# Retention over running streams: state blocks of two sequences, grouped query-state products and stores from GpSimd's queue

## The chip, the core and the metric

The kernel runs on one core of one Trainium2 chip. The metric is the device time of one execution in microseconds (us), the median of several runs. The core has a matrix engine (TensorE, PE in the profile, with its weight loads as PEld), VectorE (DVE), ScalarE (ACT), GpSimd (POOL) and SyncE (SP, which here only issues DMAs), and 16 DMA engines that all queues share.

## What is computed

The reference is one inference step of a two-layer streaming trunk. Layer 0 is multi-scale retention, layer 1 a gated spatial unit, and each is followed by a gated ConvFFN. There are 512 prompt rows of one new stream and 16 rows each of 8 running streams (the samples), 640 rows in all, with 1024 features. The change lies in the retention alone, 4 heads with keys of 256 and values of 512. Every sample has a running state S of 256 x 512 for each head; its part of one head is

```
scores = einsum('blhd,bshd->bhls', q, k) * intra
o = einsum('bhls,bshe->blhe', scores, v)
o = o + einsum('blhd,bhde->blhe', q * q_dec, S)
S = S * exp(L * log_gamma) + einsum('blhd,blhe->bhde', k * k_dec, v)
```

The third line is the query-state product, the fourth makes the new state, which is an output (ret_sample), as is the new state of the prompt (ret_prompt).

## The kernel before

Activations are held transposed (features on partitions), the rows split into a half of 384 and one of 256. Every weight block is loaded, cut into two exact parts (wh by ScalarE, wl by VectorE, `split_w`, line 63) and multiplied in three passes. `retention` (line 507) goes through four heads. For each head it makes queries and keys (`ret_qk`), values (`ret_v`), the inner part (`ret_inner`, line 642), the gate (`ret_gate`, line 738, whose products carry the name prow, as those of `ret_v` do), turns the result (`ret_turn`, pyT) and multiplies it by the output weights (`ret_out`, pxA and pxB). Blocks of the conditioning vectors (`ada`, tile pada, line 297) are put in between, one or two with each weight block.

`ret_inner` first makes the samples' scores times values (into the PSUM bank pos) and the prompt's new state in two halves (pS, copied to so at line 665, stored at 666). Then come four rounds, one for each pair of `par` (odd or even sequences) and `dt` (half of the keys). A round handles four sequences:

- it loads four state blocks of 128 x 512 (256 KB each, line 675) into tiles s0 (s in the profile);
- it adds four query-state products to pos (line 678), each with 32 columns of stationary queries, to partitions 0, 32, 64 or 96 of the same bank; the matrix engine is used in four column tiles of 128 x 32 there;
- for each pair of sequences it multiplies 48 rows of keys by values (psn, line 695; the operands st were stored to DRAM as sk and sv and loaded again in another layout, lines 689 and 690), and VectorE updates the state in place (line 696);
- each new state is stored (line 697), from SP's queue;
- one block of the prompt's attention follows (psc, then pr, ph and pl, then po).

The tiles s0 and so share one group of five buffers, so a load waits until the store of the state that used its buffer has landed. An update in place also waits until the query-state product has read the tile.

Nothing in the source fixes the order of instructions on an engine. The framework orders every engine's instructions when the program is built, by the dependences and its own estimates, and the engine then executes them in that order; so the products of a round stand between products of the gate. In this order PE stands at a wait, with all that is behind it. SP issues all loads and, before the change, all of these stores, in one order too.

Of the kernel before, what the change touches and what calls it, by code (L numbers as in the profile page):

```python
# [23 lines left out]
T = 16  # L24
# [12 lines left out]
class Trunk:  # L37
# [25 lines left out]
    def split_w(self, src, kt, cols, eng=None):  # L63
        """Load a weight block and cut it into two exact f32r parts."""
        n = kt * cols
        self.trickle(self.rates.pop(0) if self.rates else self.rate)
        raw = self.ahead.pop(0) if self.ahead else self.load_w(src, kt, cols)
        hi = self.wp.tile([128, 1024], F32R, tag="wh", name="wh")
        lo = self.wp.tile([128, 1024], F32R, tag="wl", name="wl")
        self.nc.scalar.copy(hi[:, :n], raw[:, :n])  # L70
        (eng or self.nc.vector).tensor_tensor(lo[:, :n], raw[:, :n], hi[:, :n].bitcast(F32), op=ALU.subtract)  # L71
        v = lambda t: t[:, :n].rearrange("p (k c) -> p k c", k=kt)
        return v(hi), v(lo)
# [12 lines left out]
    def w8(self, w, c0, cols=256):  # L86
        """A [1024, cols] column block of w as 8 K-tiles of (hi, lo)."""
        out = []
        for kh in range(2):
            hi, lo = self.split_w(w[kh * 512:(kh + 1) * 512, c0:c0 + cols], 4, cols)  # L90
            out += [(hi[:, k], lo[:, k]) for k in range(4)]
        return out
# [17 lines left out]
    def mm3(self, out, w, h, start, stop):  # L110
        """One K-tile of a product with stationary w, in three exact-part passes."""
        self.mm(out, w[0], h[0], start, False)
        self.mm(out, w[0], h[1], False, False)
        self.mm(out, w[1], h[0], False, stop)

    def mm3_ws(self, pA, pB, w, h, start, stop):
        """The same for both row halves."""
        whi, wlo = w
        hAh, hAl, hBh, hBl = h
        self.mm(pA, whi, hAh, start, False)  # L120
        self.mm(pB, whi, hBh, start, False)
        self.mm(pA, whi, hAl, False, False)
        self.mm(pB, whi, hBl, False, False)
        self.mm(pA, wlo, hAh, False, stop)
        self.mm(pB, wlo, hBh, False, stop)

# [1 line left out]
    def setup(self):  # L128
# [10 lines left out]
        # per-feature vectors as per-partition columns  # L139
# [14 lines left out]
        with self.tc.tile_pool(name="setup", bufs=1, reuse_waits="tile") as sp:  # L154
# [71 lines left out]
            def after(h, d0):  # L226
                """K-tiles d0 and d0 + 1 of the first queries and keys, first row half."""
# [22 lines left out]
    def ada_pair(self, dp, pool):  # L250
        """Shift and scale of the first sub-layer for two column tiles."""
# [26 lines left out]
    def ada(self, l, m):  # L278
        """Conditioning vectors of 2048 features, as steps of one weight block each."""
# [40 lines left out]
    def square(self, half, d, quick=False):  # L320
        """Adds the squares of column tile d of x to the running sum of a half."""
# [12 lines left out]
    def norm_rstd(self, half):  # L334
        """rstd of each row of a half, rows on partitions: [128, blocks]."""
# [14 lines left out]
    def norm(self, l, which, lazy=None, after=None):  # L350
        """h = rmsnorm(x) * A + B per feature and sequence, as exact f32r parts.

        Returns the result lists and a function that emits one row half."""
# [92 lines left out]
    def residual_b(self, l, gbase, d, pB, final=True):  # L446
# [5 lines left out]
        t = self.tp.tile([128, 128], F32, tag="rest", name="rest")  # L452
# [10 lines left out]
    # row block rb of h, K-tile k: (hi, lo) stationary operands  # L463
# [5 lines left out]
    def proj_rows(self, h, w, rb):  # L469
        """Row-layout product of row block rb with a [1024, 256] weight block."""  # L470
        pb = self.bank("prow")
        for k in range(KD):
            hh, hl = self.hrow(h, k, rb)
            whi, wlo = w[k]
            self.mm(pb[:, :256], hh, whi, k == 0, False)
            self.mm(pb[:, :256], hh, wlo, False, False)
            self.mm(pb[:, :256], hl, whi, False, k == KD - 1)
        return pb

    def proj_cols(self, h, w, i):  # L480
        """Transposed product with column tile i of a [1024, 256] weight block."""
# [7 lines left out]
    def proj_half(self, h, w, i, half):  # L489
        """The same for one row half."""  # L490
# [8 lines left out]
    def proj_set(self, h, ws, split):  # L499
        """Column tiles of several blocks; with split, all first halves come first."""  # L500
# [38 lines left out]
    def ret_first(self, h):  # L539
        """Rotated queries and keys of the first head, from products begun before."""  # L540
# [10 lines left out]
    def ret_qk(self, h, base, hd):  # L551
        """Rotated queries or keys of a head, transposed."""
# [20 lines left out]
    def ret_v(self, h, hd, between):  # L573
        """Values of a head in row layout, as exact f32r parts."""
# [15 lines left out]
    def ret_probs(self, hd, dtab, pb, n, c0):  # L590
        """Decayed scores in exact f32r parts."""
# [9 lines left out]
    def ret_keys(self, hd, k, dt, sk):  # L601
        """Decayed k rows, for one half of d, in exact f32r parts."""
# [20 lines left out]
    def ret_prep(self, hd, qk):  # L623
        """What the samples and the states need of queries and keys alone."""
# [4 lines left out]
        # samples: scores, and the decayed queries for the running states  # L629
# [12 lines left out]
    def ret_inner(self, hd, qk, v, prep):  # L642
# [12 lines left out]
        # the prompt state, one half of d at a time  # L655
        for dt in range(2):
# [7 lines left out]
            so = rp.tile([128, DV], F32, tag="s0", name="so", bufs=5)  # L664
# [5 lines left out]
        for rnd in range(4):  # L670
            par, dt = divmod(rnd, 2)
            s0 = []
            for i in range(4):
                t = rp.tile([128, DV], F32, tag="s0", name="s0", bufs=5)
                nc.sync.dma_start(t, io["state_ret"][0, 2 * i + par, hd, dt * 128:(dt + 1) * 128, :])
                s0.append(t)
            for i in range(4):
                nc.tensor.matmul(
                    pos[32 * i:32 * i + 32, :], self.qd[:, dt, 2 * i + par, :], s0[i], start=False, stop=True,
                    skip_group_check=True,  # L680
                )
            for pair in range(2):
# [8 lines left out]
                for i in range(2):  # L691
                    b = 2 * (2 * pair + i) + par
                    t = s0[2 * pair + i]
# [3 lines left out]
                    nc.sync.dma_start(io["ret_sample"][0, b, hd, dt * 128:(dt + 1) * 128, :], t)  # L697
            # prompt: block i of queries against key blocks i, i - 1, ..., 0
# [39 lines left out]
    def ret_gate(self, h, hd, o, last):  # L738
# [6 lines left out]
        for n, (e, rb) in enumerate(order):  # L745
# [9 lines left out]
            else:  # L755
                sg = rp.tile([128, 256], F32, tag="sg", name="sg", bufs=5)
# [5 lines left out]
    def ret_turn(self, hd, o):  # L762
        """Gated output of a head, transposed, in exact f32r parts; one row half a call."""
# [22 lines left out]
    def ret_out(self, l, hd, yT, turn, mid):  # L786
        """Adds the head's share of the output product."""
# [27 lines left out]
    def down(self, l, gbase, w, tiles, mid):  # L815
        """x += gate * (tiles^T w): tiles are [128, 640] f32, split just before use."""
# [14 lines left out]
        for d0, nd in ((0, 2), (2, 3), (5, 3)):  # L831
# [21 lines left out]
            # the last K-tiles: all of the first row half, then the second  # L853
# [104 lines left out]
    def conv_out(self, l):  # L958
        """The last raw rows of each sequence, transposed back."""
# [14 lines left out]
    def sgu(self, l, h, emit, mid):  # L974
# [16 lines left out]
        with self.tc.tile_pool(name="gp", bufs=1, reuse_waits="tile") as gp:  # L991
            # masked mixing matrices, transposed; block-diagonal ones for the samples
# [15 lines left out]
            # v in row layout  # L1008
# [137 lines left out]
def _tables():  # L1146
    """Constants that depend on the shapes alone."""
# [50 lines left out]
```

## Time and profile before

| | |
|---|---|
| median of 3 runs | 2327.37 us (2323.67 to 2332.08) |
| span of the profiled execution, first to last instruction | 2326.8 us |
| mean granted clock of TensorE | 0.988 |
| PE busy | 2239.1 us (96%) |
| PEld, DVE, ACT, POOL busy | 2086.2, 1227.8, 861.7, 432.9 us |
| DMA | 252.86 MB, mean 109 GB/s |

Of the profiled execution only the span is given, not a time of its own; the median of the runs is 0.6 us above the span. In the rows, x64 is a count of instructions, the number after "|" is the time in which at least one of them was running, then the mean of one in ns, then the idle time of the engine just before them with what ended it. A 32-bit float product, as those into pos, psc and pada are, shows as two records each; one on exact parts (prow, psn, po) shows as one. Starts and durations of a matmul are in us; the end is modelled, so the start of the next instruction says more than the duration.

### The profile page before, as it was taken

To read this page: it belongs to the slowest core of one execution; us is meant where nothing else is said; L and a number is where in the kernel's file an instruction comes from. 1 tells how busy PE (TensorE), PEld (TensorE's weight loads), DVE (VectorE), ACT (ScalarE), POOL (GpSimd) and SP (SyncE) were. 2 spreads that over 40 slices of the span, in tenths; PEclk is the share of its full clock that TensorE was granted. 3 is DMA by queue.
4 is the path that set the end of the run, shared out by engine and by line. 5 is a ranking of instruction groups with operands and counts; after the bars stand their busy time and mean duration, and the time that the engine had idled before them with its cause. 6 is when DMAs were issued, how large, how long until landed. Compare 5 with 4: busy or idle time off the path is not lost. (4 is left out here: it accounts for less than half of the span.)

```text
span 2326.8 us, 39734 instructions
## 1 busy us (share of the span) xinstructions
PE 2239.1 (96%) x15832; PEld 2086.2 (90%) x15832; DVE 1227.8 (53%) x2458; ACT 861.7 (37%) x1783; POOL 432.9 (19%) x695
## 2 busy tenths in 40 slices
PE   6999999999999999999999999699999999999998
PEld 5868968969968999999999999699999899999998
DVE  5425426326338544446656336953655664445753
ACT  4312212212214544445544222122544454445544
POOL 3201001001004322212012002770001232222010
PEclk9999999999999999999999999899999999999999
DMA  8465454262352343444322222342122122222221
GB/s 277 133 204 173 151 190 132 73 197 87 98 178 89 118 145 129 136 145 130 89 75 65 92 73 71 71 98 75 55 73 74 61 92 73 73 80 73 73 70 59
DMA packets 193009, 252.86 MB, mean 109 GB/s; under 512 B 11648, under 2 KB 158064, under 8 KB 192824
## 3 DMA queue, kind: packets, MB, share of 16 engines
q1 hardware_dynamic: 190616, 245.35, 33.1%
q0 software_dynamic: 2208, 4.98, 1.4%
q8 instruction: 124, 2.03, 0.4%
q14 instruction: 61, 0.50, 0.1%
HBM read 221.65 MB, written 28.60 MB: 108 GB/s over the span
## 5 line engine op out<-in xcount | busy, mean ns | idle before, releaser
L71 DVE TENSOR_TENSOR wl<-wr,wh 128x1024 fp32r<-128x1024 f32 (+1 forms) x284 | 351.5, 1238 | 217.1 <-ACT wh L70 214.4
L70 ACT CAST wh<-wr 128x1024 fp32r<-128x1024 f32 (+1 forms) x286 | 284.7, 995 | 434.3 <-PE pB L61 175.2
L61 PE MATMUL pA<-hi,wh 128*128 128x384 f32 x1024 | 353.5, 345 | 0.3 <-ACT hi L425 0.3
L61 PE MATMUL pA<-lo,wh 128*128 128x384 f32 x1024 | 349.0, 341 | 1.5 <-POOL lo L427 1.5
L61 PE MATMUL pA<-hi,wl 128*128 128x384 f32 x1024 | 348.2, 341 | 0.0
L61 PE MATMUL prow<-wh,hi 128*128 128x256 f32 x1072 | 306.4, 287 | 1.0 <-ACT wh L70 0.8
L61 PE MATMUL prow<-wh,lo 128*128 128x256 f32 x1072 | 305.9, 286 | 0.1
L61 PE MATMUL prow<-wl,hi 128*128 128x256 f32 x1072 | 305.8, 286 | 0.0
L61 PE MATMUL pB<-lo,wh 128*128 128x256 f32 x1024 | 287.7, 281 | 1.3 <-DVE lo L427 1.2
L61 PE MATMUL pB<-hi,wh 128*128 128x256 f32 x1024 | 287.0, 281 | 0.4 <-DVE rt L569 0.2
L61 PE MATMUL pB<-hi,wl 128*128 128x256 f32 x1024 | 286.6, 280 | 0.0
L61 PEld LDWEIGHTS prow<-wh,hi 128*128 128x128 f32 x1072 | 204.6, 191 | 19.4 <-issue 16.4
L61 PEld LDWEIGHTS prow<-wl,hi 128*128 128x128 f32 x1072 | 205.1, 191 | 16.6 <-issue 16.0
L61 PEld LDWEIGHTS prow<-wh,lo 128*128 128x128 f32 x1072 | 205.2, 191 | 16.1 <-issue 15.5
L61 PEld LDWEIGHTS pA<-hi,wh 128*128 128x128 f32 x1024 | 194.1, 190 | 10.5 <-issue 5.8
L61 PEld LDWEIGHTS pA<-lo,wh 128*128 128x128 f32 x1024 | 194.0, 189 | 3.1 <-POOL lo L427 2.5
L61 PEld LDWEIGHTS pB<-lo,wh 128*128 128x128 f32 x1024 | 193.6, 189 | 2.8 <-DVE lo L427 2.1
L61 PEld LDWEIGHTS pA<-hi,wl 128*128 128x128 f32 x1024 | 193.4, 189 | 1.4 <-issue 0.5
L61 PEld LDWEIGHTS pB<-hi,wh 128*128 128x128 f32 x1024 | 193.4, 189 | 1.0 <-DVE rt L569 0.4
L61 PEld LDWEIGHTS pB<-hi,wl 128*128 128x128 f32 x1024 | 193.3, 189 | 0.0
L61 PE MATMUL dA<-ghi,wh 128*128 128x384 f32 x544 | 185.3, 341 | 0.0
L61 PE MATMUL dA<-ghi,wl 128*128 128x384 f32 x544 | 184.6, 339 | 0.0
(227 smaller groups left out, 4293.2 us busy)
## 6 DMA issues: line engine op xcount, KB each, us to landing
wr<-in_ffn_w_up SPq DMA_DIRECT2D x88, 512.0 KB
wa<-in_w_ada SPq DMA_DIRECT2D x80, 512.0 KB
wr<-in_ret_w_in SPq DMA_DIRECT2D x48, 512.0 KB
wr<-in_sgu_w_in SPq DMA_DIRECT2D x48, 512.0 KB
wr<-in_ffn_w_down SPq DMA_DIRECT2D x44, 384.0 KB
s<-in_state_ret SPq DMA_DIRECT2D x64, 256.0 KB
out_ret_sample<-s SPq DMA_DIRECT2D x64, 256.0 KB
wr<-in_sgu_w_out SPq DMA_DIRECT2D x24, 384.0 KB
```

Source lines behind the costliest of these rows:

```text
L61: self.last_mm = self.nc.tensor.matmul(out, l, r, start=start, stop=stop).ins
L70: self.nc.scalar.copy(hi[:, :n], raw[:, :n])
L71: (eng or self.nc.vector).tensor_tensor(lo[:, :n], raw[:, :n], hi[:, :n].bitcast(F32), op=ALU.subtract)
```

## The change

- The four state blocks of a round become two tiles of 128 x 2 x 512 (512 KB each), one load for two sequences. Their group has three buffers; so moves to the shared group t2.
- The four query-state products are written with sequence 2 first, then 3, and 0 and 1 are held behind 3 on PE by an added dependence (`issue_after`).
- The new states of a pair are stored by one DMA, from GpSimd's queue.
- Two buffers are taken away elsewhere (rest 2 to 1, sg 5 to 4). All else in the diff is comments, left out here.

```diff
@@ residual_b
-        t = self.tp.tile([128, 128], F32, tag="rest", name="rest")
+        t = self.tp.tile([128, 128], F32, tag="rest", name="rest", bufs=1)
@@ ret_inner
-            so = rp.tile([128, DV], F32, tag="s0", name="so", bufs=5)
+            so = self.tp.tile([128, DV], F32, tag="t2", name="so", bufs=3)
...
             s0 = []
-            for i in range(4):
-                t = rp.tile([128, DV], F32, tag="s0", name="s0", bufs=5)
-                nc.sync.dma_start(t, io["state_ret"][0, 2 * i + par, hd, dt * 128:(dt + 1) * 128, :])
+            part = lambda a, pair: a[0].rearrange("(p i two) h d e -> p two h d i e", two=2, i=2)[
+                pair, par, hd, dt * 128:(dt + 1) * 128
+            ]
+            for pair in range(2):
+                t = rp.tile([128, 2, DV], F32, tag="s0", name="s0", bufs=3)
+                nc.sync.dma_start(t, part(io["state_ret"], pair))
                 s0.append(t)
-            for i in range(4):
-                nc.tensor.matmul(
-                    pos[32 * i:32 * i + 32, :], self.qd[:, dt, 2 * i + par, :], s0[i], start=False, stop=True,
-                    skip_group_check=True,
-                )
+
+            def read_state(i):
+                return nc.tensor.matmul(
+                    pos[32 * i:32 * i + 32, :], self.qd[:, dt, 2 * i + par, :], s0[i // 2][:, i % 2], start=False,
+                    stop=True, skip_group_check=True,
+                ).ins
+
+            read_state(2)
+            with self.tc.issue_after(read_state(3)):
+                read_state(0)
+                read_state(1)
...
                 for i in range(2):
-                    b = 2 * (2 * pair + i) + par
-                    t = s0[2 * pair + i]
+                    t = s0[pair][:, i]
                     pb = self.sbank("psn")
                     self.mm(pb, st[pair][:, i, dt * 128:(dt + 1) * 128], st[pair][:, i, DK:], True, True)
                     nc.vector.scalar_tensor_tensor(t, t, g16, pb, op0=ALU.mult, op1=ALU.add)
-                    nc.sync.dma_start(io["ret_sample"][0, b, hd, dt * 128:(dt + 1) * 128, :], t)
+                nc.gpsimd.dma_start(part(io["ret_sample"], pair), s0[pair])
@@ ret_gate
-                sg = rp.tile([128, 256], F32, tag="sg", name="sg", bufs=5)
+                sg = rp.tile([128, 256], F32, tag="sg", name="sg", bufs=4)
```

The built programs show how the order moves. On PE, second head, first round, before: the third and the fourth product of the round (pos from an s0 tile and the queries qd), with products of the gate (prow, from parts wh, wl of the weights and hi, lo of the activations) between them.

```order
L678 MATMUL pos_3155<-s0_3217,qd_922 32x512
L61 MATMUL prow_3536<-wh_3504,lo_793 128x256
L61 MATMUL prow_3536<-wh_3504,hi_800 128x256
L61 MATMUL prow_3536<-wl_3505,hi_800 128x256
L61 MATMUL prow_3536<-wh_3504,lo_801 128x256
L61 MATMUL prow_3563<-wh_3498,hi_321 128x256
L61 MATMUL prow_3563<-wl_3499,hi_321 128x256
L678 MATMUL pos_3155<-s0_3219,qd_922 32x512
L61 MATMUL prow_3563<-wh_3498,lo_322 128x256
```

After the change, on PE in the second head, its first round and then its second:

```order
L609 MATMUL pk_3153<-ident_75,qk_2744 128x128
L683 MATMUL pos_3131<-s0_3191,qd_922 32x512 x2
L683 MATMUL pos_3131<-s0_3189,qd_922 32x512
L609 MATMUL pk_3157<-ident_75,qk_2744 128x128 x4
L683 MATMUL pos_3131<-s0_3189,qd_922 32x512
L61 MATMUL prow_3460<-wh_3450,hi_321 128x256
```

```order
L61 MATMUL prow_3515<-wh_3456,lo_801 128x256
L683 MATMUL pos_3131<-s0_3234,qd_922 32x512 x2
L683 MATMUL pos_3131<-s0_3232,qd_922 32x512 x2
L61 MATMUL prow_3542<-wh_3450,hi_836 128x256
```

In the first round of a head three products now stand together and the fourth behind four transposes (pk), ahead of the prompt's second state half; in the other three rounds all four stand together. Over the four heads the order before has 56 products alone and 4 pairs; now it has 12 groups of four, 4 of three and 4 alone. Of the 64 psn products, 28 stood alone and 18 in pairs; now 40 stand alone and 12 in pairs.

On SP, second head, before, from the end of the first round to the third (s0 loads, ret_sample stores, st operands):

```order
L697 DMA out_ret_sample<-s0_3217 128x512
L697 DMA out_ret_sample<-s0_3219 128x512
L675 DMA s0_3268<-in_state_ret 128x512
L697 DMA out_ret_sample<-s0_3262 128x512
L697 DMA out_ret_sample<-s0_3264 128x512
L697 DMA out_ret_sample<-s0_3266 128x512
L675 DMA s0_3309<-in_state_ret 128x512
L675 DMA s0_3311<-in_state_ret 128x512
L697 DMA out_ret_sample<-s0_3268 128x512
L675 DMA s0_3313<-in_state_ret 128x512
L675 DMA s0_3315<-in_state_ret 128x512
L689 DMA st_3321<-sk_2964 48x2x128 x2
```

and after, the same stretch:

```order
L679 DMA s0_3234<-in_state_ret 128x2x512
L679 DMA s0_3273<-in_state_ret 128x2x512
L699 DMA st_3281<-sk_2940 48x2x128 x2
L700 DMA st_3281<-sv_3127 48x2x512
L699 DMA st_3281<-sk_2940 48x2x128 x2
L679 DMA s0_3275<-in_state_ret 128x2x512
L700 DMA st_3281<-sv_3127 48x2x512
L679 DMA s0_3363<-in_state_ret 128x2x512
L78 DMA wr_3813<-in_ret_w_in 128x4x256
L679 DMA s0_3365<-in_state_ret 128x2x512
```

The stores are gone from between the loads. The loads of a head's first round and half of its second now stand in the head before it (in the first head ahead of its first conditioning blocks). The st operands of the third round stand ahead of one of that round's state loads.

On POOL, second head, after: the last two of a head's eight stores and the gate's products (o times sg) behind them.

```order
L706 DMA out_ret_sample<-s0_3363 128x2x512
L706 DMA out_ret_sample<-s0_3365 128x2x512
L769 TENSOR_TENSOR o_3122<-o_3122,sgs_3485 128x256
L769 TENSOR_TENSOR o_3122<-o_3122,sg_3635 128x256
L769 TENSOR_TENSOR o_3123<-o_3123,sgs_3485 128x256
```

Before, the gate's products on POOL had no DMA ahead of them in the retention. In the order of the other layers the two programs agree apart from a few neighbours that change places.

## Rows read from the trace of the kernel before

**Rows 1.** The page: its first line and PE's busy time.
```profile
span 2326.8 us, 39734 instructions
PE 2239.1 (96%) x15832; PEld 2086.2 (90%) x15832; DVE 1227.8 (53%) x2458; ACT 861.7 (37%) x1783; POOL 432.9 (19%) x695
```

**Rows 2.** By stretch: window, length, PE PEld DVE ACT POOL busy, clock, DMA, GB/s.
```profile
120.00:700.00 580.00, 568.45 (x3667) 463.39 (x3666) 251.77 (x551) 123.51 (x223) 42.57 (x45) 1.00 0.46 147
```

**Rows 3.** Groups of PE's instructions: the query-state products.
```profile
L678 PE MATMUL pos<-s,qd 128*32 128x512 f32 x128 | 63.6, 611 | 0.0
```

**Rows 4.** Timeline of PE (start, length): a product alone, then a pair.
```profile
131.55 0.28 PE L61 MATMUL prow<-wh,hi 128*128 128x256 f32 x1
131.76 1.05 PE L678 MATMUL pos<-s,qd 128*32 128x512 f32 x2
132.74 0.39 PE L61 MATMUL prow<-wl,hi 128*128 128x256 f32 x1
132.96 0.28 PE L61 MATMUL prow<-wh,lo 128*128 128x256 f32 x1
133.08 0.28 PE L61 MATMUL prow<-wh,hi 128*128 128x256 f32 x1
...
129.87 1.05 PE L678 MATMUL pos<-s,qd 128*32 128x512 f32 x4
130.85 0.38 PE L61 MATMUL prow<-wl,hi 128*128 128x256 f32 x1
```

**Rows 5.** Timeline of PE: conditioning products in four column tiles, between others.
```profile
257.32 0.28 PE L61 MATMUL pB<-hi,wl 128*128 128x256 f32 x1
257.53 1.07 PE L297 MATMUL pada<-wa,sT 128*32 128x256 f32 x16
258.53 0.39 PE L61 MATMUL prow<-wh,hi 128*128 128x256 f32 x1
258.75 0.28 PE L61 MATMUL prow<-wl,hi 128*128 128x256 f32 x1
```

**Rows 6.** Timeline of PE around 24 conditioning records and two query-state products.
```profile
154.53 0.28 PE L61 MATMUL prow<-wh,lo 128*128 128x256 f32 x1
...
157.70 0.28 PE L61 MATMUL prow<-wl,hi 128*128 128x256 f32 x1
```

**Rows 7.** Timeline of PE: one psn product alone, prow ahead of it and behind.
```profile
143.47 0.28 PE L61 MATMUL prow<-wh,lo 128*128 128x256 f32 x1
143.68 0.50 PE L61 MATMUL psn<-st 48*128 48x512 f32 x1
...
144.33 0.28 PE L61 MATMUL prow<-wl,hi 128*128 128x256 f32 x1
```

**Rows 8.** Waits of PE in the inner part: total, times, longest.
```profile
PE psn L61 <- DMA st<-sv: 8.7, 4, 2.7
```

**Rows 9.** Timeline of SP's queue (issue times), and PE's first psn behind it.
```profile
123.41 0.33 SPq L690 DMA_DIRECT2D st<-sv  x1
...
131.67 0.95 SPq L697 DMA_DIRECT2D out_ret_sample<-s  x2
132.68 1.73 SPq L675 DMA_DIRECT2D s<-in_state_ret  x2
...
127.94 0.73 PE L61 MATMUL psn<-st 48*128 48x512 f32 x2 [2.65 <-DMA st<-sv]
```

**Rows 10.** Waits of SP's queue over the span.
```profile
SPq L697 <- DVE s L696: 111.9, 48, 8.6
```

**Rows 11.** DMA issues from POOL's queue: size each, median us from issue to landing.
```profile
out_sgu_v<-vt POOLq DMA_DIRECT2D x24, 64.0 KB, 1.9
vr<-in_final_g POOLq DMA_DIRECT2D x1, 4.0 KB, 5.7
```

**Rows 12.** Timeline of DVE: two updates of a state in place.
```profile
130.96 1.29 DVE L696 SCALAR_TENSOR_TENSOR s<-s,psn 128x512 f32<-128x512 f32 x2 [9.01 <-PE pos L678]
```

**Rows 13.** Busy time by stretch behind a wait of the second head (clock after the busy times).
```profile
304.00:307.40 3.40, 3.40 (x11) 1.60 (x9) 0.69 (x1) 0.00 (x0) 0.00 (x0) 0.53 0.41 151
```

## The prediction

> **What bounds the kernel now.** I read the page first: PE is busy 2239.1 of 2326.8 us [rows 1]. Then busy time by stretch: from 120 to 700 us, which holds the inner part of all four heads, PE is busy 568.45 of 580 us, at full clock and with DMA at 0.46 [rows 2]. So only 11.6 us can be won there by removing waits, and 8.7 of these are one wait, the first psn of each head for its operands st [rows 8]. Whatever else the change wins must be work taken off PE. The third view is the groups of PE's instructions: the 64 query-state products (128 records) hold PE for 63.6 us [rows 3]. The fourth is PE's timeline, to see what one of them costs the stream.
>
> **The price of a product and of a group.** Around a lone product [rows 4], prow starts at 131.55 and the second prow behind it at 132.96, 1.41 us apart; with nothing between, two steps of prow take 2 x 0.12 (132.96 to 133.08). So a lone product costs 1.17 us, 0.98 to the next start and some 0.2 for the change of tile shape on either side. Two standing together start their successor 0.98 later as well (129.87 to 130.85) [rows 4]: the second product of a pair is free, because it runs in another column tile. The trace of before has no four of them. The nearest row is the conditioning block, also 32-bit with 32 columns, four products to a group and moving data of 256: two such groups, 16 records, are by columns what one group of four with 512 would be. From pB at 257.32 to the second prow at 258.75 is 1.43, less two steps of 0.12 each, 1.19 us [rows 5]. Bounds for a group of four: 1.17 (as one) to 2.34 (as two pairs). I take 1.20, since the conditioning block shows four tiles at once.
>
> **The change part by part.**
>
> 1. *Grouping.* Before, by the order: 56 alone and 4 pairs. Two of the 56 stand inside a conditioning block: 154.53 to 157.70 is 3.17, less 0.24 for prow and 1.66 for 24 conditioning records (1.5 times 0.98, and 0.19) leaves 1.3 for both [rows 5, 6]. So before: 54 x 1.17 + 4 x 1.18 + 1.3 = 69.2 us. After: 12 groups of four x 1.20, 4 of three x 1.19, 4 alone x 1.17 = 23.8 us. Difference **-45.4 us**. All of it is PE's own time in a stretch where PE is 98% busy.
> 2. *psn.* Six pairs are split. One alone costs 0.62 (143.47 to 144.33 less 0.24) [rows 7]; the split of a pair costs between nothing and another 0.62 each. I take the middle, 0.35: **+2.1 us** (0 to 3.7).
> 3. *New waits for state blocks.* In rounds two to four of a head, a load needs a buffer whose store has landed, and the store needs the update, which needs the group before. From one group's start to the next: the group 1.05, two updates 1.29 [rows 12], the store from POOL's queue, the load. PE's own work from the third group to the fourth of the second head is, counted in the order, 36 prow at 0.12, 6 psc and 9 po products at some 0.25 each, three psn at 0.62 and the group at 1.20: 4.3 + 3.8 + 1.9 + 1.2 = 11.2 us. The store's landing from POOL's queue is 1.9 us for 64 KB, and 5.7 at the kernel's start behind eight other DMAs [rows 11]; none of 512 KB is shown. On SP a 256 KB store issued at 131.67 had landed for the second load, out by 134.41: under 2.7 us [rows 9]. For the load the upper bound is the 4.5 us of st, issued 123.41 and awaited until 127.94 [rows 9], the lower the 2 us of the smallest store. I take 3 us each, nearest to the 256 KB store: the chain is 1.05 + 1.29 + 3 + 3 + 0.5 for the issues = 8.8, against 11.2. With both upper ends it is 1.05 + 1.29 + 5.7 + 4.5 = 12.5 and PE waits 1.3 us, twelve times 16 us. What covers the chain is the gate's prow in PE's order; if that runs out, each us is PE's. For updates that queue behind VectorE's other work I book 0.25 for each of twelve groups: **+3.0** (0 to 16). The Trainium skill (DMA: Bandwidth & Descriptors, Anatomy of one DMA) gives a DMA from GpSimd 2.0 us and its bytes at 436 GB/s, 3.2 us for 512 KB as an estimate; with it the chain would be 9.0 and the sum the same. No row here shows it.
> 4. *st of the third round.* Its buffer is free only after the last psn of round two; three DMAs are issued (0.43 each) and about 5 us of PE's order lie between. With 2 us to land there is room, with the 4.5 of st [rows 9] a wait of 0.8 each. I book 0.3 x 4: **+1.2** (0 to 3.3).
> 5. *The first psn.* Three products now stand ahead of it, so PE arrives 1.5 us later, while its operands are some 0.6 to 1.2 later too, since pk, of which they are made, is delayed. I take a quarter of the 8.7 us away [rows 8]: **-2.2** (0 to -8.7).
> 6. *Moved queues.* SP loses 64 stores, before which it waited 111.9 us for updates [rows 10] with weight loads behind; the only large wait of PE there is for st [rows 8], so this is worth nothing now. SP gains waits for the landing of stores, with loads of weights behind them; cover are three weight buffers. POOL gains 32 issues, and the gate's products behind the last store of a head: POOL is busy 42.57 of 580 us [rows 2]; they wait for the group norm, which follows the last round anyway. The buffers taken from sg, rest and t2 are reused by one engine in order or after far longer than they are held: nothing; if an so store were late, the round's probabilities would wait 1 us, in a head once.
>
> Sum: -45.4 + 2.1 + 3.0 + 1.2 - 2.2 = -41.3 us. Made against the span of 2326.8, that is 2285.5; the median of the runs is 0.6 above that span, so **2286 us**. The rest of the kernel is in the same order and PE-bound; I expect it unchanged.
>
> **Rivals.**
> - *Waits take part of the gain.* The chain of item 3 is near its upper ends, because the store comes from another queue and loads are twice as large. For: the 5.7 us of a load from POOL's queue [rows 11]; and a head's eight loads and eight stores of 512 KB run beside its weights. Against: DMA is at 0.46 [rows 2]. A wait of 1.3 us at each of 12 groups and 3.3 in item 4 instead of 4.2 booked: 2286 + 15 = 2301. A wait can also lower the clock: behind the second head's wait for st the granted clock stood at the lower level, 0.53 over 3.4 us [rows 13], half of which is lost, 1.7 us.
> - *Further products are cheap, not free.* Four column tiles that read four different moving tiles overlap in part only, and each product behind the first adds something. For: the four of the conditioning block move less each [rows 5]. Against: the pair adds nothing to the next start [rows 4]. At 0.1 us for each of the 3 products behind the first in twelve groups, and of the 2 in four, 44 x 0.1 = 4.4: 2290. The Trainium skill (TensorE: Matmul & The Clock Gate, Why this matters for your kernels) gives three small-column products of 512 a speed-up of only 2.38, by which, as an estimate, three would take 1.26 times one, some 0.13 more for each further product. No row here shows three.
> - *Groups run two at a time.* Moving data of four different tiles might not be read at once at 512 columns. For: no such row. Against: four tiles at once in the conditioning block [rows 5]. Twelve groups cost 2.2 instead of 1.2, the threes 1 us more: 16 us, 2302.
> - *The change doesn't group.* If waits between the two tiles or transposes split every group in two, PE does 32 pieces instead of 20 and 12 x 1.17 = 14 us are lost, 2300; to lose the gain whole it would take 35 more pieces, which the order excludes.
> - *Slower.* One mechanism: the store from GpSimd's queue lands so late that PE stands at each of the twelve groups, and the clock falls behind it. It decides where a wait exceeds (41.3 + 3.0) / 12 = 3.7 us with the 1.7 of the clock in it, so 2.0 us of standing: a chain of 13.2, with the load at 3 a store of 7.4 us. No row reaches that; 5.7 is the most. At 9 us each wait is 3.6 + 1.7 and the time 2286 - 3 + 64 = 2347.
>
> **How the numbers follow.** Forecast 0.69 (2277 to 2295: all costs of items 2 to 4 at nothing and half of 8.7 won is 2277, items 2 and 4 at their upper ends and half of the first upper end of item 3 is 2295); cheap, not free 0.05 (about 2290); waits 0.13 (2295 to 2315); two at a time or split 0.06 (about 2301); slower 0.04; no change 0.03. The range 2277 to 2302 holds about 0.85. From no change a measurement of this kernel can tell about 0.3%, 7 us: faster 0.93, same 0.03, slower 0.04.
>
> **What would show it.** In the profile after: PE's busy time for pos near 21 us; groups of four with 0.98 to 1.0 to the next start; PE waits in the inner part near 11 us in all, the one for st under 8.7; PE's busy time about 43 us lower in total; the stage from 700 on as long as before. It is wrong if a row "PE pos <- DMA s" stands among PE's waits with over 10 us, if a group takes 2 us, or if the later layers change by more than 3 us.

## The result and the profile after

The changed kernel takes 2289.43 us (median of 4 runs, 2286.31 to 2295.55), the kernel before 2329.72 us in the same session (4 runs, 2323.67 to 2334.96). The ratio is 0.9825 (95% interval 0.981 to 0.9839), 40.3 us less. The two profiled executions differ by 37.2 us. Each trace here is of one execution, and the four of the changed kernel differ by 9 us among themselves, so a few us between two traces say little alone. The forecast was 2286 us, the range 2277 to 2302.

The page after; it answers to [rows 1]. PE's busy time fell by 40.1 us.

```profile
span 2289.6 us, 39641 instructions
PE 2199.0 (96%) x15832; PEld 2079.7 (91%) x15832; DVE 1233.2 (54%) x2458; ACT 862.2 (38%) x1783; POOL 454.1 (20%) x727
```

The group of the query-state products, which answers to [rows 3], and three of PE's waits up to the end of the retention (total, times, longest), of which the first two answer to [rows 8]:

```profile
L683 PE MATMUL pos<-s,qd 128*32 128x512 f32 x128 | 21.2, 605 | 6.6 <-DMA s<-in_state_ret 6.6
...
PE pos L683 <- DMA s<-in_state_ret: 6.6, 5, 2.3
...
PE psn L61 <- DMA st<-sv: 3.7, 5, 1.6
...
PE pxA L61 <- ACT yT L787: 1.3, 1, 1.3
```

The same 128 records hold PE for 21.2 us instead of 63.6. A wait for the state loads is new; the wait for st has shrunk from 8.7 us.

To see which part of the program gained, the span is cut where the last pxB product of the retention starts: at 737.45 us before and 704.24 us after. Busy time by stretch (start and end, length, then PE, PEld, DVE, ACT and POOL, clock, DMA share, GB/s), first of the kernel before:

```profile
120.00:737.45 617.45, 603.95 (x3900) 497.12 (x3899) 280.68 (x629) 138.99 (x253) 56.18 (x59) 1.00 0.44 141
737.45:2326.80 1589.35, 1539.11 (x10821) 1504.98 (x10819) 885.18 (x1683) 679.15 (x1441) 342.24 (x586) 0.99 0.29 89
```

and after the change:

```profile
120.00:704.24 584.24, 567.93 (x3902) 497.31 (x3903) 282.46 (x628) 140.17 (x254) 76.90 (x90) 0.99 0.45 146
704.24:2289.60 1585.36, 1535.13 (x10821) 1499.76 (x10819) 888.77 (x1684) 678.47 (x1441) 342.76 (x587) 0.99 0.29 89
```

The retention is 33.2 us shorter, the layers behind it 4.0 us, with the same 10821 PE records. I put these 4.0 us down to the clock, not to the change; the last section gives the reasons. In the retention PE stood idle 13.5 us before (617.45 - 603.95) and 16.3 us after.

PE's timeline after, for a group of three in a head's first round, and a group of four in its second (start, length):

```profile
117.31 1.06 PE L683 MATMUL pos<-s,qd 128*32 128x512 f32 x6
118.30 0.66 PE L609 MATMUL pk<-ident,qk 128*128 128x128 f32 x4
...
136.93 1.06 PE L683 MATMUL pos<-s,qd 128*32 128x512 f32 x8
137.92 0.38 PE L61 MATMUL prow<-wh,lo 128*128 128x256 f32 x1
```

Three products start their successor 0.99 us later and four 0.99 us later. One alone took 0.98 [rows 4].

Three stretches of the retention ran at the lower clock level, where before had one [rows 13]. By stretch again, the clock is the first number behind the busy times:

```profile
166.00:172.60 6.60, 6.60 (x26) 5.28 (x25) 4.65 (x12) 1.43 (x2) 1.64 (x3) 0.50 0.67 255
459.90:466.40 6.50, 6.50 (x26) 5.33 (x24) 1.97 (x5) 0.35 (x2) 1.48 (x2) 0.50 0.75 245
671.20:674.70 3.50, 3.12 (x12) 3.03 (x13) 2.84 (x5) 1.17 (x2) 0.00 (x0) 0.51 0.66 171
```

At half the clock, half of each stretch is lost: 3.3 + 3.2 + 1.7 = 8.2 us, against 1.6 us before. The third stands behind the wait of 1.3 us for yT above, the first behind a wait for a state load, the second behind a wait for st:

```profile
164.46 1.07 PE L683 MATMUL pos<-s,qd 128*32 128x512 f32 x8 [2.27 <-DMA s<-in_state_ret]
...
458.19 0.73 PE L61 MATMUL psn<-st 48*128 48x512 f32 x2 [1.62 <-DMA st<-sv]
```

Where does the wait of 2.27 us come from? The queues of SP and POOL ahead of it, and the time from issue to landing of the one store that POOL issues at 152.82 (last row):

```profile
151.61 0.36 SPq L291 DMA_DIRECT2D wa<-in_w_ada  x1
152.06 0.39 SPq L78 DMA_DIRECT2D wr<-in_ret_w_in  x1
153.09 0.34 SPq L291 DMA_DIRECT2D wa<-in_w_ada  x1
160.79 0.37 SPq L679 DMA_DIRECT2D s<-in_state_ret  x1
...
152.82 0.72 POOL L706 DMA_DIRECT2D out_ret_sample<-s  x1 [10.53 <-DVE s L705]
...
out_ret_sample<-s POOLq DMA_DIRECT2D x1, 512.0 KB, 7.9
```

SP sends two weight blocks of 512 KB ahead of the store and one behind it. The store lands after 7.9 us, where the median of the 32 is 3.4. Only then, at 160.79, does SP issue the load into the same buffer, and the group waits for it until 164.46.

### The profile page after: what moved, and what is told of

Same layout as the page of the kernel before. It is cut to its first block, busy times and chain, and to the rows that moved or that the text cites. A ratio compares the mean times of both kernels' runs of the same rounds, so it can differ in the third digit from the quotient of the medians.

```text
span 2289.6 us, 39641 instructions
## 1 busy us (share of the span) xinstructions
PE 2199.0 (96%) x15832; PEld 2079.7 (91%) x15832; DVE 1233.2 (54%) x2458; ACT 862.2 (38%) x1783; POOL 454.1 (20%) x727
```

## The experiments

All ratios are to the kernel before, measured in the same session.

What each of the three parts does by itself was open: the grouping order, the blocks of two, GpSimd's queue. The first four runs take the grouping alone, blocks alone and the queue alone, and measure what a group costs without column tiles.

**Grouping alone** (on the kernel before).

```diff
-            for i in range(4):
-                nc.tensor.matmul(
...
+            read_state(2)
+            with self.tc.issue_after(read_state(3)):
+                read_state(0)
+                read_state(1)
```

> The kernel before with one edit: the four products of a round are written 2, 3, then 0 and 1 behind 3, as in the change; single tiles, five buffers and stores from SP stay. In its order the 64 query-state products stand in 31 pieces (15 alone, 15 of three, 1 of four) where before has 60. Theory (what costs is a piece, 1.17 us, whatever stands in it): 29 x 1.17 = 34 us less than before, ratio about 0.985, a little more if waits for the last tile's buffer come in (five buffers, four of them in use): 0.985 to 0.990. Rival (without blocks and a third buffer of 512 KB the loads come too late, and waits eat the gain): ratio over 0.993 and a row of PE waits on s loads of over 15 us.

Measured: 0.9932 (0.9917 to 0.9947), 2316.65 us. Neither theory. The products took what the pieces say (58.1 us to the next starts before, 33.8 here, with 31 pieces), but PE's waits grew, and not at the state loads. Three rows of the inner part, and the stretch that answers to [rows 2]:

```profile
PE psn L61 <- DMA st<-sv: 9.4, 4, 2.7
PE po L61 <- ACT ph L597: 5.5, 2, 4.3
PE pos L678 <- DMA s<-in_state_ret: 1.1, 2, 0.9
...
120.00:700.00 580.00, 558.08 (x3700) 473.46 (x3700) 256.48 (x563) 128.16 (x231) 44.84 (x48) 0.97 0.47 149
```

PE stood idle 21.9 us of these 580, 10 more than before. Six stretches ran at the lower clock level, some 30 us in all, of which half, 15 us, was lost, against 1.6 before. So in this trace, the slowest of the four runs, most of the 30 us of PE work that the grouping saved went to waits and to the clock: the retention ends at 730.56 us, 6.9 us sooner than before. By the medians 16 us were gained, so about half was lost. Why ph came so late (4.3 us, once) was not followed up.

**Blocks alone** (the change without its order and without GpSimd's queue).

```diff
-            read_state(2)
-            with self.tc.issue_after(read_state(3)):
-                read_state(0)
-                read_state(1)
+            for i in range(4):
+                read_state(i)
...
-                nc.gpsimd.dma_start(part(io["ret_sample"], pair), s0[pair])
+                nc.sync.dma_start(part(io["ret_sample"], pair), s0[pair])
```

> The change without its order and without GpSimd's queue: blocks of two sequences, products written 0 to 3, stores from SP. In its order the products stand in 33 pieces (10 alone, 19 pairs, 4 of four). Theory (pieces): 27 x 1.17 = 32 us less than before, ratio 0.986 (0.984 to 0.990). Rival (the order alone makes the gain, blocks by themselves give none): ratio 0.997 to 1.003. Second rival (512 KB loads and stores on SP's one queue make PE wait): over 0.993, with waits of PE on s of over 12 us.

Measured: 0.9825 (0.9807 to 0.9842), 2291.94 us, as much as the whole change. One load brings two sequences, so the framework puts their two products side by side unasked, and 33 pieces are left of 60. Three of PE's waits in the inner part (the longest other one is 2.3 us in all, po for pl), and the stretch up to the last pxB:

```profile
PE psn L61 <- DMA st<-sv: 2.2, 4, 0.9
PE pxA L61 <- ACT yT L785: 1.3, 1, 1.3
PE pos L683 <- DMA s<-in_state_ret: 1.2, 2, 0.7
...
120.00:702.11 582.11, 573.35 (x3900) 491.98 (x3899) 280.51 (x628) 139.85 (x253) 54.18 (x58) 1.00 0.47 147
```

PE works 5.4 us longer there than after the change (573.35 against 567.93) and stands idle only 8.8 us, against 16.3; no stretch of the retention was at the lower clock. So in the two traces the change's 13 pieces fewer, some 15 us, were paid back: 7.5 us in waits, and 8.2 in the slow clock that its busy time contains.

**GpSimd's queue alone** (on the kernel before; `nc.sync.dma_start` of each new state becomes `nc.gpsimd.dma_start`).

> The kernel before with one edit: the 64 stores of 256 KB go from GpSimd's queue. In its order the products stand in 62 pieces (60 before). Theory (SP's 111.9 us of waiting for updates cost nothing, since PE hardly waits for what SP loads): ratio 0.998 to 1.003, two pieces more are 2.3 us. Rival (the stores block SP's loads, and moving them is worth part of the gain): ratio under 0.996. Second rival (a store from GpSimd lands later and PE waits for buffers): over 1.004 with a row of PE waits on s.

Measured: 1.0012 (1.0003 to 1.0022). As the theory has it: SP's 111.9 us of waiting [rows 10] cost the kernel before nothing, and the queue in itself brings nothing. A store of half the size took 2.4 us to land:

```profile
out_ret_sample<-s POOLq DMA_DIRECT2D x64, 256.0 KB, 2.4
```

**One column tile.** All four products of a round go to partitions 0 to 31.

```diff
-                    pos[32 * i:32 * i + 32, :], self.qd[:, dt, 2 * i + par, :], s0[i // 2][:, i % 2], start=False,
+                    pos[0:32, :], self.qd[:, dt, 2 * i + par, :], s0[i // 2][:, i % 2], start=False,
```

> The change with all four products of a round put into the same 32 partitions of the bank (the result of sequences 1 to 3 goes to the rows of sequence 0, so the products are all made but not where they belong). Its order has 12 groups of four, 4 pairs and 8 alone. Theory (a second product is free only because it runs in another column tile): every product costs 0.98 to the next start, and a piece 0.2 once: a group of four about 4.1 us instead of 1.2, in all 40 us more than the change, time near that of before, ratio to before 0.998 to 1.003. Rival (what makes a group cheap is that the tile shape changes once, and the products behind the first stream at the pace of other products): a group of four 1.2 + 3 x 0.25, ratio about 0.987; by this the change's gain would not need column tiles.

Measured: 0.9985 (0.9972 to 0.9997), 2329.89 us: by the two ratios some 37 us more than the change, as the theory says. A group of four in one tile (start, length) and what follows it:

```profile
141.85 3.62 PE L683 MATMUL pos<-s,qd 128*32 128x512 f32 x8
145.40 0.50 PE L61 MATMUL psn<-st 48*128 48x512 f32 x1
```

Without separate column tiles the next product starts after 3.55 us instead of 0.99, and the whole gain is gone. Standing together saves little; running in four tiles saves the time. In this run the four products also add into the same 32 rows of the bank, which was not separated from the tile; prow's products add into the same rows too, and follow each other at 0.12 us [rows 4].

The second session asked which part makes the waits for states: the queue or the grouping.

**Stores from SP** (the change with `nc.sync` in place of `nc.gpsimd` for the new states).

> The change with one edit: the new states are stored from SP's queue. In its order the products stand in the same 20 pieces as in the change. Theory 1 (the queue makes the waits: in the change a store of 512 KB from GpSimd's queue, free to leave while SP fetches weights, took up to 7.9 us to land, and PE stood 6.6 us at state loads with two clock falls of 3.4 us behind; blocks with stores from SP, 33 pieces, showed neither): no row of PE waits on s over 2 us, and against plain_blocks 13 pieces x 1.17 = 15 us less: ratio to before 0.974 to 0.978. Theory 2 (grouping makes the waits, since PE comes to a group as soon as the order lets it and needs all four states at once): the waits on s stay at 5 us and more, and the ratio at 0.981 to 0.985, as the change.

Measured: 0.978 (0.9766 to 0.9795), 2279.75 us; the interval lies below that of the change. Theory 1 holds, at the upper edge of its range. PE's two waits for DMAs in the inner part, and the stretch up to the last pxB:

```profile
PE psn L61 <- DMA st<-sv: 4.2, 4, 1.7
PE pos L683 <- DMA s<-in_state_ret: 1.4, 1, 1.4
...
120.00:691.08 571.08, 561.10 (x3904) 492.59 (x3904) 278.88 (x629) 139.92 (x255) 51.74 (x58) 1.00 0.48 150
```

Waits on s fell from 6.6 to 1.4 us, and the retention ends at 691.1 instead of 704.2. SP's queue at the same place in the program as the late store above:

```profile
153.17 0.39 SPq L706 DMA_DIRECT2D out_ret_sample<-s  x1
153.66 0.41 SPq L291 DMA_DIRECT2D wa<-in_w_ada  x1
156.16 0.38 SPq L706 DMA_DIRECT2D out_ret_sample<-s  x1
156.63 0.42 SPq L679 DMA_DIRECT2D s<-in_state_ret  x1
```

Here SP waits for the update, sends the store and only then the weights; the buffer's next load goes out at 156.63, so the store had landed in under 3.5 us, not 7.9. SP's wait for the updates, which I had listed as a queue relieved, keeps the weights behind the store.

**No grouping** (the change with the four products written 0 to 3, stores from GpSimd's queue).

> The change with one edit: the products are written 0 to 3 and none is held behind another. In its order they stand in 32 pieces (8 alone, 20 pairs, 4 of four). Theory 1 (GpSimd's queue makes the waits): waits on s of over 4 us and clock falls in the retention stay, and 12 pieces x 1.17 = 14 us more on PE than the change: ratio to before 0.986 to 0.990. Theory 2 (grouping makes the waits): hardly a wait on s, and the time of blocks with stores from SP, ratio 0.981 to 0.984.

Measured: 0.9842 (0.9828 to 0.9856). By the time, between the two; by the trace, theory 2: one wait on s, and no stretch of the retention at the lower clock.

```profile
PE pos L683 <- DMA s<-in_state_ret: 0.5, 1, 0.5
```

The stores landed no sooner (median 3.8 us). So the waits need both parts: PE stood 6.6 us on s with grouping and GpSimd's stores, 1.4 with grouping alone, 0.5 with GpSimd's stores alone, and 1.2 with neither. Against the change the time is not clearly different; the grouping, worth 14 us of PE time there, brought little with GpSimd's stores. Against blocks alone, with stores from SP, it brought about 10 us (0.9825 to 0.978).

**First round whole** (first with GpSimd's stores, then with SP's):

```diff
-            read_state(2)
+            if rnd == 0:
+                with self.tc.issue_after(self.last_mm):
+                    read_state(2)
+            else:
+                read_state(2)
```

> The change with one edit: in a head's first round the first product is held behind the last matmul of the prompt's second state half, and so all four stand together. In its order there are 16 groups of four and nothing else. Theory (pieces): 4 x 1.17 = 4.7 us less than the change, ratio to before 0.979 to 0.982. Rival (the first group comes some 3 us later, so its updates and stores do, and what is won comes back as waits on s in the second and third round): ratio 0.982 to 0.986.

> Both edits: stores from SP and the first round's four products together; 16 groups of four, and of the psn products 30 alone and 17 pairs. Theory 1 of the stores with the theory of pieces: 17 x 1.17 = 20 us less than blocks alone, ratio to before 0.972 to 0.977, faster than both kernels. Theory 2: as first_whole, 0.979 to 0.984.

Measured: 0.9841 (0.9821 to 0.9862) and 0.9792 (0.9779 to 0.9806). The theory of pieces missed both times; the rivals' ranges held, but not by their mechanism. With GpSimd's stores the waits on s hardly grew (6.9 us against 6.6), and those for st doubled (7.9 against 3.7), in a trace that is the slowest of its four runs. With stores from SP the waits on s were 1.1 us, and the large one was the row

```profile
PE psn L61 <- DMA st<-sv: 5.8, 4, 1.9
...
296.00:304.00 8.00, 8.00 (x30) 6.48 (x31) 3.15 (x6) 0.68 (x2) 0.00 (x0) 0.50 0.61 211
```

and stretches at the lower clock such as this one, behind a 1.89 us wait for st at 295.90; in the whole retention they cost some 10 us, against 1.7 with stores from SP alone.

The third session takes ScalarE's queue, leaves stores out, and goes after the wait for st.

**Stores from ScalarE's queue** (`nc.scalar` in place of `nc.gpsimd`).

> The change with one edit: the new states are stored from ScalarE's queue, which like SP's is served by hardware, but like GpSimd's is free of SP's order. In its order the products stand in the same 20 pieces; of the psn products 46 stand alone (40 in the change, 30 with stores from SP). Theory 1 (the late landing lies in GpSimd's queue itself, whose 512 KB stores took 3.1 us at best and 7.9 at worst): waits of PE on s under 2 us in all, ratio to before 0.977 to 0.981. Theory 2 (it lies in the order: stores that SP doesn't wait for let SP fetch weights first, and the store shares the DMA engines with them): the waits on s stay at 4 us and more, ratio 0.981 to 0.986.

Measured: 0.9812 (0.9797 to 0.9828), waits on s 2.7 us: between the theories. The store at the disputed place, issued from ScalarE, and the load that waits for its landing:

```profile
151.44 0.46 ACTq L706 DMA_DIRECT2D out_ret_sample<-s  x1
...
158.45 0.37 SPq L679 DMA_DIRECT2D s<-in_state_ret  x1
```

The load went out 7.0 us after the store, which had run beside the same weight loads. So GpSimd's queue is not needed for the late landing there; what both late cases have, and stores from SP lack, is weights sent just ahead of the store. No run moved the weights alone. PE came later to the groups (0.47 us of wait at this one), so the verdict by the total stays open.

**Three quarters of the stores left out** (of the new states only those of a head's last round are stored).

> The change with the new states of a head stored in its last round only; those of the first three rounds are made and not stored, so 3/4 of the output ret_sample is missing and a buffer comes free with the update. In its order the products stand in 22 pieces. Theory (PE's waits on s are the landing of stores): no wait on s over 1 us, ratio to before 0.974 to 0.979. Rival (the loads are late for another reason: issued behind weights on SP, or 512 KB each): waits on s of 4 us and more, ratio 0.981 to 0.986.

Measured: 0.9779 (0.9764 to 0.9794), and among PE's waits there is no row for s at all. So without the landings no wait on s is left; as the loads go out sooner too, this doesn't say which of the two, store or load, was late. It is no faster than stores from SP, in a trace that lost 3.4 us to the clock behind a wait for st; so those stores cost PE a few us at most.

**Samples' values first**, with stores from SP: the rows of the samples, from which sv and st are made, are multiplied first in `ret_v`.

```diff
-            for rb in range(5):
+            for rb in (4, 0, 1, 2, 3):
```

> The change with stores from SP, and the values of the samples' rows made first instead of last, so that the operands st can land earlier. 20 pieces; of the psn products 52 stand alone and 6 in pairs, and the first psn stands some 1.7 us earlier in PE's order. Theory (the 4.2 us of waits on st with stores from SP come from the last store of the values): waits on st under 1 us and no clock fall behind them, against some 3 us for eleven more psn pieces: ratio 0.976 to 0.979. Rival (what was won at st is lost at the loads of the states, since the groups follow each other sooner): waits on s of over 4 us, ratio 0.979 to 0.983.

Measured: 0.9783 (0.9769 to 0.9797). The wait for st is gone from the list; a new one of 3.4 us (PE pk behind the copy so, in the first head alone) and the lower clock behind it took its place, and eleven more psn pieces. The theory's range held, but the kernel is no faster than with stores from SP alone (0.978).

**Samples' values first and first round whole**, stores from SP.

> As sp_v4, and the first round's four products together: 16 groups of four, 40 psn alone and 12 in pairs. With stores from SP alone this grouping had cost 5.8 us of waits on st and 10 us of clock falls behind them. Theory (those waits were for st, so they go): ratio 0.971 to 0.976, the fastest of all. Rival (the first group behind the prompt's state delays updates, stores and loads): waits on s of over 4 us, ratio 0.978 to 0.983.

Measured: 0.9761 (0.9747 to 0.9775), 2276.48 us: at the theory's upper edge, the fastest kernel of the study by its median, 0.65% below the change. All its four runs lie below the four of the run before it; the interval overlaps that of stores from SP. Its longest waits and the stretch up to the last pxB:

```profile
PE pk L609 <- ACT so L665: 3.8, 1, 3.8
PE pxA L61 <- ACT yT L791: 1.3, 1, 1.3
PE pos L683 <- DMA s<-in_state_ret: 1.1, 3, 0.4
...
120.00:686.10 566.10, 560.71 (x3909) 492.76 (x3910) 282.88 (x631) 141.24 (x256) 54.60 (x58) 1.00 0.47 150
```

PE idles 5.4 us of 566. The first-round edit, which brought nothing over stores from SP alone (0.9792 against 0.978), brings 0.2% once the wait for st is gone.

## Why the prediction was right, and where it was off

The time lay in the range and 3 us from the forecast. The mechanism, further products free beside the first, held; that the number came so close is luck in part, as the sum below shows. In the retention of the two traces, by the prediction's items:

- **Grouping, -45.4.** Right: pieces of four and of three cost 0.99 to the next start. The rival of cheap, not free products and that of two at a time fall with that row, and the one-tile run shows that standing together is not enough, which leaves the column tiles as the cause. The Trainium skill (TensorE: Matmul & The Clock Gate, Measured speedup vs the span model) has a speed-up of 2.38 for three column tiles of 512; here three products took the time of one.
- **psn, +2.1.** One alone costs 0.62 us and a pair 0.86 in both traces, so splitting six pairs cost 6 x 0.38 = 2.3.
- **Waits for state blocks, +3.0.** The term that was too small. They were 6.6 us, and the clock behind the longest took another 3.3. The step that failed is the 3 us taken for each landing, of the store and of the load. The longest wait, 2.3 us, in the first head's fourth round, is the store's: the stores landed in 3.4 us by the median, but this one in 7.9, and its neighbour in 7.0. Item 3 held 5.7 us for the most that a row shows; the view that it read has a load of 6.0 as well. The runs with stores from SP and from ScalarE point to the weights that, no longer held back by SP's stores, ran beside it; item 6 had counted the unblocked SP as worth nothing.

  The other four waits, 4.4 us together, stand in the third round of each head, and there the load was late: the stores ahead of it landed in 3.2 to 4.1 us, but from the load's issue to the group were 6.8, 6.6, 5.5 and 5.9 us, where 4.5 was the upper end. The first of them, between loads of the same round's st, and the stretch in which it ran, with the DMA engines busy to 0.93:

```profile
142.23 0.95 SPq L699 DMA_DIRECT2D st<-sk  x2
143.27 0.74 SPq L679 DMA_DIRECT2D s<-in_state_ret  x1
...
150.09 1.07 PE L683 MATMUL pos<-s,qd 128*32 128x512 f32 x8 [1.60 <-DMA s<-in_state_ret]
...
143.30:150.10 6.80, 5.20 (x33) 3.73 (x33) 1.30 (x3) 0.97 (x2) 0.00 (x0) 1.00 0.93 283
```

  In all four heads SP issues five of the round's six st loads ahead of that state load, and with stores from SP only one; there the same group of the first head started 4.7 us after the load's issue (144.32), without a wait. Whether the st loads alone made it late was not tried. The upper sum of item 3 also leaves out the 0.5 us for issues that its first sum has: with it the chain is 13.0, the wait 1.8 us, twelve times 22. The Trainium skill (DMA: Bandwidth & Descriptors, Anatomy of one DMA) gives 3.2 us for such a store, as an estimate; the median agrees, and the late ones are not in it.
- **st of the third round, +1.2, and the first psn, -2.2.** Together -1.0; the wait for st in fact fell by 5.0 (8.7 to 3.7), the lone large part of the sum that came out better. The first psn carried it: in the four heads it now stands 0.6, 0.8, 1.6 and 0.2 us, 3.2 in all, where it stood 1.8 to 2.7 each. The third round waited once:

```profile
480.40 0.70 PE L61 MATMUL psn<-st 48*128 48x512 f32 x2 [0.48 <-DMA st<-sv]
```

- **The clock.** Only the rivals had it. The stretches at the lower level took 8.2 us in the retention against 1.6, so 6.6 more.

The sum, with the grouping as forecast and the rest as measured: -45.4 + 2.3 + 2.8 (idle time 13.5 to 16.3) + 6.6 = -33.7, and the retention ends 33.2 us sooner. PE's busy time there bears out the part without idle time: it fell by 36.0 us, against -45.4 + 2.3 + 6.6 = -36.5. The forecast for the retention was -41.3, 8 us more than came. That the profiled total came closer is the 4.0 us of the later layers, and that the medians came closer still (40.3) the spread of single runs, 2286 to 2296: both are luck. Of the prediction's three signs of being wrong one came true: the later layers changed by 4.0 us, where 3 was its limit.

What the prediction could not see is in the experiments: the forecast took the three parts as one. Blocks without grouping and without GpSimd's queue give the same time, since most of the grouping's further 15 us goes to waits and clock when the stores go from GpSimd's queue. "Moved queues: nothing" holds for the kernel before (1.0012) and not for the change, where it is worth some 10 us (0.9825 against 0.978). The rival of slower, PE standing at each of twelve groups, did not come: five waits, the longest 2.3 us. One store of 32 passed the 7.4 us that it asked of each.

## What to carry to other kernels

When small products run in separate column tiles, one at a time and four at a time cost the same PE time, so load the operands in pieces that let them become ready together. A queue that waits is not always a loss: SP's wait for the updates kept 512 KB weight loads behind the store whose landing freed the next buffer, and most st loads stood behind the state load; before moving a DMA to a free queue, look at what the old queue will send ahead of it. When an edit that should save work doesn't, look at the waits of PE by name and at the clock behind each, and remove the wait before giving up the edit.

## What was not expected of the hardware

- **The same wait is followed by a lower clock in one execution and not in another.** In the later layers both programs have PE waits of 1.81 us for ghi. In the trace of before the clock fell behind the one that ended at 1190.07; after the change the same instruction waited 1.81 us at 1157.04 and the clock stayed up.

```profile
1190.07 0.38 PE L61 MATMUL dB<-ghi,wh 128*128 128x256 f32 x1 [1.81 <-ACT ghi L826]
...
1191.20:1195.20 4.00, 4.00 (x19) 4.00 (x19) 2.92 (x9) 1.78 (x6) 0.99 (x2) 0.57 0.52 66
```

```profile
1157.04 0.39 PE L61 MATMUL dB<-ghi,wh 128*128 128x256 f32 x1 [1.81 <-ACT ghi L835]
```

  Four such stretches (at 744, 1191, 1768 and 2253 us) stand in the later layers of before, with no counterpart after, and one after (at 1436 us) with none before; at half the clock each costs up to 1.7 us, so the three more cost up to 5.1. Over the kernels of this study the same layers took 1584.8 to 1592.8 us. So I put the 4.0 us there down to the clock, not to the change. In the retention the stretches of the change stood behind waits of 2.3, 1.6 and 1.3 us, but other waits of 1.6 us (150.09, 322.55) had none behind them, nor had three waits for st of 2.1 to 2.7 us in the kernel before. What decides it no run here shows.
- **A store's landing depends on what runs beside it.** 512 KB took 3.1 to 7.9 us from GpSimd's queue, and 7.0 from ScalarE's at the place of the 7.9. In those 7.9 us all DMAs moved 2.5 MB (311 GB/s), in the 3.1 us of a quick one (338.39) 0.7 MB (220 GB/s).
- **Products of one column tile that follow each other** cost 0.86 us each behind the first ((3.55 - 0.98) / 3), a little less than a lone one.
